# MLP weights split into high and low parts by two casting loads from GpSimd's queue

## Chip, core and metric

The kernel runs on one core of one Trainium2 chip. The metric is the device time of one execution in microseconds (us). Five engines work side by side, each through its own queue in order: TensorE (PE; its weight loads appear as PEld), VectorE (DVE), ScalarE (ACT), GpSimd (POOL) and SyncE (SP), which here only issues transfers (DMAs).

## What is computed

A trunk of two layers over 528 tokens (16 meta tokens and 512 of the input) of 1024 features. Each layer is a mixer (layer 0: retention and gated DeltaNet heads; layer 1: Mamba-2) followed by a squared-ReLU MLP with 4096 hidden features, each closed by a layer norm. The change is in the MLP:

```python
def sq_relu_mlp(h, w1, w2):
    return jnp.square(jax.nn.relu(h @ w1)) @ w2
...
    for i in range(DEPTH):
        ...
        h = layer_norm(DN_ALPHA * h + mix, ln1_w[i], ln1_b[i])
        h = layer_norm(DN_ALPHA * h + sq_relu_mlp(h, mlp_w1[i], mlp_w2[i]), ln2_w[i], ln2_b[i])
    return h[:, N_META:]
```

All inputs and the output are float32.

## The kernel before

Every large product is made of three matmuls in the float32r format (`mm3`): weight and activation are each held as a rounded high part and a low part that is the remainder, and high times high, high times low and low times high are added in PSUM.

**Weights.** They lie in HBM as tiles of 128 x 1024 float32 (512 KB): eight blocks of 128 x 128 side by side. `fetch` loads a tile from SP's queue into a raw buffer `wr` (2 buffers). `split` then makes the parts: ACT copies the raw tile with rounding into `wh`, and DVE subtracts that from the raw tile into `wl`. This goes by halves of 512 columns; `wh` and `wl` have 6 such halves each, which is three weight tiles. So SP is ahead of TensorE by up to two raw tiles and three split ones.

**The MLP.** `mlp` goes through the 4096 hidden features in four chunks of 1024. A chunk is a phase of eight `w1` tiles (each gives 128 hidden features for all tokens, f = 0 to 7), then a phase of eight `w2` tiles (each adds to 128 output features, m = 0 to 7). Two layers of four chunks of sixteen tiles are 128 weight tiles. Layer 0 works on 272 + 256 tokens as two halves, one PSUM tile `pmm` each; layer 1 works on 512 tokens in one. After a `w1` product `evac_u` takes it out for each half: ACT applies the ReLU (L381), GpSimd squares it in float32 (L383), ACT squares it with rounding into the high part (L389), DVE subtracts for the low part (L390). After a `w2` product DVE alone adds to the residual (L363, or L367 and L368).

**Ends of an MLP.** Its first three `w1` tiles (`head=3`) and its last three `w2` tiles (`tail=3`) are held together: the first half of the tokens goes through all three, and then the second half, so that the layer norm before or after can work on one half at a time. The layer norm ahead of the MLP uses GpSimd too: for a power of -0.5 (L147) and for the low parts `hl` of six of its eight feature tiles (L341).

**Order.** A tile scheduler sets the order of the instructions on each engine when the program is built, and adds the waits. In the queue of an engine nothing passes an instruction that waits. The weights of the mixers come through `wload` as well, and share the buffers `wh` and `wl` with the MLP.

Of the kernel before, what the change touches and what calls it, by code (L numbers as in the profile page):

```python
# [12 lines left out]
F32 = mybir.dt.float32  # L13
F32R = mybir.dt.float32r
# [4 lines left out]
P = 128  # L19
# [38 lines left out]
def trunk(ctx: ExitStack, tc: tile.TileContext, a, out):  # L58
# [7 lines left out]
    def nm(p):  # L66
        count[0] += 1
        return f"{p}{count[0]}"
# [23 lines left out]

    # ---------------------------------------------------------------- interleaving
    # The large products are cut into units; between two units every pending task (a generator) emits
    # its next stage, so that the tensor engine works on while other engines prepare a stage's inputs.
    tasks = []
# [29 lines left out]

    # ---------------------------------------------------------------- constants
    cst = one("cst", C_COLS)
# [20 lines left out]

    # ---------------------------------------------------------------- weights  # L150
    def split(dst_hi, dst_lo, src):
# [8 lines left out]
    def wload(src, n=1024, raw=None):  # L160
        if raw is None:
            raw = fetch(src, n)
        res = []
        for i in range(0, n, 512):
            c = min(512, n - i)
            hi = sb.tile([P, 512], F32R, tag="wh", bufs=6, name=nm("wh"))
            lo = sb.tile([P, 512], F32R, tag="wl", bufs=6, name=nm("wl"))
            split(hi[:, :c], lo[:, :c], raw[:, i:i + c])
            res.append((hi, lo))
        return res  # L170

    def mm3(o, w, x, first, last):
# [4 lines left out]
    def product(o, blks, xs, m=P, k0=0, k1=None, every=8):  # L177
        """o[m, n] += sum over k0 <= k < k1 of blks[k]^T xs[k]"""
        per = 512 // P if m == P else 8
        n = len(xs)  # L180
        for k in range(k0, k1 or n):
            hi, lo = blks[k // per]
            c = (k % per) * m
            mm3(o, (hi[:, c:c + m], lo[:, c:c + m]), xs[k], k == 0, k == n - 1)
            if k % every == every - 1 and k < n - 1:
                tick()

    def phase(tiles, rhs, evac, ns, head=0, tail=0, ready=None):
        """tiles: list of (srcs, key[, m]); rhs[half][k] = (hi, lo) APs, rhs[2] both halves where they fit a
        bank. In the first and the last tiles the halves are apart, so that what precedes and follows can  # L190
        work on one half at a time."""
        def both(blks, key):
            o = pm(512)
            product(o, blks, rhs[2], every=4)
            for hf in range(2):
                evac(key, hf, o[:, hf * 256:hf * 256 + 256])
            tick()

        def run(hf, blks, key, m=P):
            o = pm(ns[hf], part=m)  # L200
            product(o, blks, rhs[hf], m=m)
            evac(key, hf, o)
            tick()
        n = len(tiles)
        for i0, i1 in [(0, head)] + [(i, i + 1) for i in range(head, n - tail)] + [(n - tail, n)]:
            held = []
            for srcs, *key in tiles[i0:i1]:
                held.append(([b for s in srcs for b in (s if isinstance(s, list) else wload(s))], *key))
                if len(rhs) > 2 and head <= i0 < n - tail:
                    both(*held.pop())  # L210
                    continue
                if ready is not None and i0 == 0:
                    until(lambda: ready(0))
                run(0, *held[-1])
            if ready is not None and i0 == 0:
                until(lambda: ready(1))
            for args in held:
                run(1, *args)

    def jobs(lst, rhs, ns, **kw):  # L220
        """phase whose tiles bring their own evac"""
        phase(lst, rhs, lambda ev, hf, o: ev(hf, o), ns, **kw)

    # ---------------------------------------------------------------- h: hi/lo in two halves
    def htile():
        return [sb.tile([P, L], F32R, tag=f"h{kind}", bufs=8, name=nm(f"h{kind}")) for kind in "hl"]

    def parts(pair, spans):
        """(hi, lo) over the spans of both tiles"""
        return [tuple(x[:, o:o + n] for x in pair) for o, n in spans]  # L230

    # while the first loads are under way, products of zeros let the clock of the tensor engine come up
    zeros = tl("m", 272)
# [25 lines left out]
    def layernorm(r, ns, hf, go, apply, together=False):  # L259
        """statistics of the tokens of a half as its sums r come, then apply(off, bn, pt, mean, rstd, i)"""  # L260
        n = ns[hf]
# [48 lines left out]
    def norm_after(r, ns, wcol, bcol):  # L310
        """tasks for both halves, each from when its sums have been emitted"""
        res, pairs = [[], []], []
# [34 lines left out]
    def residual(hx, offs, ns, early=()):  # L347
        """evac into r = alpha * h + product"""
        r, pre = [{}, {}], [{}, {}]
# [23 lines left out]
    def mlp(l, hx, ns, ready, r, evac0):  # L373
        w1, w2 = a["mw1"], a["mw2"]
        for c in range(4):
            u = [[None] * 8 for _ in hx]

            def evac_u(f, hf, o):
# [5 lines left out]
                if hf == 0:  # L384
# [6 lines left out]

            phase([([w1[l, c * 8 + f]], f) for f in range(8)], hx, evac_u, ns,
                  head=3 if c == 0 else 0, ready=ready if c == 0 else None)
            phase([([w2[l, c, m]], m) for m in range(KT)], u,
                  lambda m, hf, o: evac0(m, hf, o, last=c == 3), ns, tail=3 if c == 3 else 0)

    # ---------------------------------------------------------------- shared pieces
    def conv_evac(cin, hf, o):
# [14 lines left out]
    def conv_job(src, wc, bcol, done):  # L413
        """projection through conv and silu, feature-major [128, L]"""
        cin = tl("s", L + 3)
        G.memset(cin[:, 0:3], 0.0)

        def evac(hf, o):
            conv_evac(cin, hf, o)
            if hf == 1:  # L420
                done(conv_silu(cin, wc, bcol))

        return [src], evac
# [21 lines left out]
    def gate_job(src, width, task):  # L445
        """small projection, then a task on its sums"""
        fm = tl("s", L, part=width)

        def evac(hf, o):
            off, n = HALF0[hf]  # L450
            S.copy(fm[:, off:off + n], o)
            if hf == 1:
                spawn(task(fm))

        return [src], evac, width

    def gate_task(fm, width):
        """token-major [128, 5, width] with unused rows zero"""
        pt = px(5 * width)
# [8 lines left out]
    def decay(dt_in, bias, alog, nh):  # L468
        """g = -exp(A_log) softplus(x + bias), sums over chunks and their exponentials"""
        n = 5 * nh  # L470
# [15 lines left out]

    # ================================================================ layer 0 mixer
    gd = {}
# [13 lines left out]

    # scratch in DRAM for the diagonal blocks of 32: a pitch of 129 rows makes the 68 blocks equidistant
    da, dt_, du = [dr.tile([17, 129, P], F32, tag=f"d{n}", bufs=1, name=f"d{n}") for n in "atu"]
# [25 lines left out]
    def gdn_keys(hd):  # L530
        yield
        yield from wait(lambda: "negc" in gd)
        f, gg, beta = kF[hd], gd["gg"], gd["beta"]
        # decays between the tokens of a chunk
        lg = tl("s", 512)
# [14 lines left out]
        V.tensor_tensor(e0, e0, triu[:16, 0:16], op=MUL)  # L550
        # similarities of the keys; the squared norms are on their diagonal
        pk = px(512)
# [31 lines left out]
    def gdn_base():  # L584
        """diagonal blocks of 32, one to a partition: forward substitution"""
        yield from wait(lambda: all(x is not None for x in AT))
# [347 lines left out]

    # ================================================================ layer 1 mixer
    lnf = sb.tile([P, 2048], F32, tag="cr", bufs=1, name="lnf")
# [26 lines left out]
    def hb(ap):  # L963
        """[128, heads] over the 64 features of a head"""
        return bc(ap, 64)
# [187 lines left out]
    hn, _, ready = norm_after(r, ns1, PP_LN + 32, PP_LN + 40)  # L1153
    # the first products begin with the groups that are ready
    until(lambda: yw[2][11] is not None)
# [19 lines left out]
    def finish(hf):  # L1175
# [16 lines left out]
        def last(blocks):  # L1192
            """both blocks at once, over the engines; what needs the mean alone comes first"""
            t = [[x[:, 0:512], x[:, 512:1024]] for x in (tl("row", 1024), tl("row", 1024))]
# [25 lines left out]

# ---------------------------------------------------------------- host side: layout only
def _tiles(w, cols):
    """[K, M] -> [M tiles, 128, K] in tiles of 128 columns"""
    k = w.shape[0]
    w = w[:, cols].reshape(k // P, P, -1, P)
    return np.ascontiguousarray(w.transpose(2, 1, 0, 3)).reshape(-1, P, k)
# [92 lines left out]
```

## Time and profile before

| | |
|---|---|
| device time, median of 3 runs | 1731.39 us (1730.09 to 1732.92) |
| span of the profiled execution, first to last instruction | 1727.4 us, 4.0 us below that median |
| TensorE busy | 1690.1 us, 98% |
| DVE, ACT, POOL busy | 1015.5, 680.0, 324.1 us |
| read from HBM | 149.95 MB, 90 GB/s over the span |
| MLP weight tiles loaded, on SP's queue | 128, from 495.4 to 1685.2 us |

The device time covers the span and what lies around it, so a sum is made against the span and 4.0 us are added for the time. Matmuls are pipelined: the duration of one is longer than the distance to the next, so the pace is read from what repeats once in a tile. The line numbers are those of the kernel before; in the changed kernel those from L164 on are ten higher (L383 becomes L393).

### The profile page before, as it was taken

The page shows a single profiled execution, that of the slowest core. Times are in us where ns is not written, and L with a number is a line of the kernel's source. Part 1 is how long each engine was busy: PE and PEld are TensorE (multiplying, and loading weights), DVE is VectorE, ACT ScalarE, POOL GpSimd, SP SyncE. Part 2 cuts the span into 40 slices and gives each one's busy share as a digit, 9 for nine tenths or more (in the row PEclk, how much of TensorE's full clock was granted, in tenths as well). Part 3 has the DMA queues.
Part 4 walks back from the last instruction along what each step waited for, and adds up shares of the span by engine and source line. Part 5 has one row for each costly group of instructions (what it writes and reads, how often), then busy time and mean ns, then how long its engine had stood idle before and what let it go on. Part 6 is the DMA issues. An engine that isn't in the chain of part 4 may idle for free.

```text
span 1727.4 us, 29456 instructions
## 1 busy us (share of the span) xinstructions
PE 1690.1 (98%) x11644; PEld 1537.0 (89%) x11644; DVE 1015.5 (59%) x2116; ACT 680.0 (39%) x1455; POOL 324.1 (19%) x380
## 2 busy tenths in 40 slices
PE   9999999999999999999999999999999999999997
PEld 8899998899999999999999878888788888888886
DVE  6896667676436443343348767868753744444345
ACT  4432345554225333242425634554432533333331
POOL 1311211010004111010202245242400411101012
PEclk9999999999999999999999999999999999999999
DMA  7224211112222222222221443333222222222221
GB/s 252 69 86 121 77 63 62 38 63 85 98 66 82 92 92 87 98 87 89 96 72 61 131 133 88 99 110 111 80 79 98 73 86 98 98 98 89 94 98 61
DMA packets 80325, 157.99 MB, mean 91 GB/s; under 512 B 12668, under 2 KB 45820, under 8 KB 79932
## 3 DMA queue, kind: packets, MB, share of 16 engines
q1 hardware_dynamic: 80044, 155.86, 28.2%
q8 instruction: 91, 1.49, 0.4%
q14 instruction: 46, 0.38, 0.1%
q10 hardware_dynamic: 144, 0.26, 0.0%
HBM read 149.95 MB, written 6.15 MB: 90 GB/s over the span
## 4 chain that ended last, share of the span: by engine, by line
PE 84%; DVE 6%; DMA 3%; POOL 3%; ACT 2%; issue 2%; SPq 0%; POOLq 0%; DVEq 0%; ACTq 0%
PE pmm L173 24%; PE pmm L175 24%; PE pmm L174 24%; DMA row<-rd 2%; DVE s L407 2%; DVE wl L153 2%; POOL row L985 1%; PE pmx L271 1%; POOL hl L341 1%; DMA wr<-in_w 1%; PE pmx L331 1%; PE pmx L1049 1%; PE pmx L1045 1%; POOL n L147 1%; PE pmx L753 1%
## 5 line engine op out<-in xcount | busy, mean ns | idle before, releaser
L173 PE MATMUL pmm<-hh,wh 128*128 128x272 f32 (+4 forms) x2104 | 652.3, 311 | 2.3 <-ACT wh L152 0.9
L174 PE MATMUL pmm<-hl,wh 128*128 128x272 f32 (+4 forms) x2104 | 638.5, 304 | 2.7 <-POOL hl L341 2.1
L175 PE MATMUL pmm<-hh,wl 128*128 128x272 f32 (+4 forms) x2104 | 640.3, 304 | 0.1
L153 DVE TENSOR_TENSOR wl<-wr,wh 128x512 fp32r<-128x512 f32 (+1 forms) x498 | 376.2, 759 | 319.8 <-ACT wh L152 313.5
L152 ACT CAST wh<-wr 128x512 fp32r<-128x512 f32 (+1 forms) x498 | 306.6, 619 | 628.3 <-PE pmm L174 605.1
L173 PEld LDWEIGHTS pmm<-hh,wh 128*128 128x128 f32 (+2 forms) x2104 | 393.5, 187 | 25.0 <-issue 4.4
L174 PEld LDWEIGHTS pmm<-hl,wh 128*128 128x128 f32 (+2 forms) x2104 | 393.6, 187 | 24.4 <-POOL hl L341 4.6
L175 PEld LDWEIGHTS pmm<-hh,wl 128*128 128x128 f32 (+2 forms) x2104 | 393.5, 187 | 17.0 <-DVE wl L153 0.3
L173 PE MATMUL pmm<-s,wh 128*128 128x256 f32 (+2 forms) x1192 | 377.9, 317 | 0.0
L175 PE MATMUL pmm<-s,wl 128*128 128x256 f32 (+2 forms) x1192 | 377.2, 317 | 0.0
L174 PE MATMUL pmm<-s,wh 128*128 128x256 f32 (+2 forms) x1192 | 376.4, 316 | 0.0
L174 PEld LDWEIGHTS pmm<-s,wh 128*128 128x128 f32 x1192 | 224.3, 188 | 15.5 <-DVE s L1124 0.3
L173 PEld LDWEIGHTS pmm<-s,wh 128*128 128x128 f32 x1192 | 224.4, 188 | 15.1
L175 PEld LDWEIGHTS pmm<-s,wl 128*128 128x128 f32 x1192 | 224.1, 188 | 15.0
L383 POOL TENSOR_TENSOR m<-m 128x256 f32<-128x256 f32 (+1 forms) x128 | 92.1, 729 | 536.0 <-ACT m L381 532.7
L147 POOL TENSOR_TENSOR n<-n,neg 128x1 f32<-128x1 f32 (+2 forms) x58 | 37.9, 657 | 462.7 <-DVE n L146 436.5
L390 DVE TENSOR_TENSOR s<-m,s 128x256 fp32r<-128x256 f32 (+1 forms) x128 | 64.3, 521 | 95.2 <-POOL m L383 93.2
L407 DVE SCALAR_TENSOR_TENSOR s<-s,pp,s 128x528 f32<-128x528 f32 x120 | 96.5, 804 | 25.8 <-ACT s L405 24.1
L363 DVE TENSOR_TENSOR m<-m,pmm 128x256 f32<-128x256 f32 (+1 forms) x108 | 43.7, 423 | 107.4 <-PE pmm L175 107.2
L381 ACT ACTIVATE m<-pmm 128x256 f32<-128x256 f32 (+1 forms) x128 | 48.7, 380 | 60.4 <-PE pmm L175 60.4
L985 POOL TENSOR_TENSOR row<-row,m 128x1024 f32<-128x1024 f32 x16 | 32.8, 2052 | 122.3 <-DMA row<-rd 78.3
L389 ACT ACTIVATE s<-m 128x256 fp32r<-128x256 f32 (+1 forms) x128 | 54.0, 422 | 3.9
(275 smaller groups left out, 1501.1 us busy)
## 6 DMA issues: line engine op xcount, KB each, us to landing
wr<-in_mw SPq DMA_DIRECT2D x128, 512.0 KB, 3.3
wr<-in_w SPq DMA_DIRECT2D x88, 512.0 KB, 3.3
wr<-in_wo SPq DMA_DIRECT2D x29, 512.0 KB, 3.5
row<-rd SPq DMA_DIRECT2D x16, 512.0 KB, 6.0
s<-rd SPq DMA_DIRECT2D x32, 128.0 KB, 6.1
out<-row SPq DMA_DIRECT2D x7, 256.0 KB, 2.0
wr<-in_wo SPq DMA_DIRECT2D x6, 256.0 KB, 3.0
dt<-row SPq DMA_DIRECT2D x3, 365.5 KB, 5.9
```

The source lines that it names most:

```text
L147: G.tensor_tensor(dst, t, neg5[0:part, 0:n], op=POW)
L152: S.copy(dst_hi, src)
L153: V.tensor_tensor(dst_lo, src, dst_hi.bitcast(F32), op=SUB)
L173: T.matmul(o, w[0], x[0], start=first, stop=False)
L174: T.matmul(o, w[0], x[1], start=False, stop=False)
L175: T.matmul(o, w[1], x[0], start=False, stop=last)
L381: S.activation(t, o, AF.Relu)
L383: G.tensor_tensor(q, t, t, op=MUL)
L389: S.activation(hi, t, AF.Square)
L390: V.tensor_tensor(lo, q, hi.bitcast(F32), op=SUB)
L407: V.scalar_tensor_tensor(acc, cin[:, k:k + L], w[k], acc, op0=MUL, op1=ADD)
L985: G.tensor_tensor(g3(rw, 8), g3(rw, 8), bc(gc[:, c * 32 + 8 * g:c * 32 + 8 * g + 8], P), op=SUB)
```

## The change

For the MLP, `wload` is replaced by a new `wcast`. It issues three instructions for a weight tile: a load from GpSimd's queue that casts the tile from HBM into `wh`; on ACT the negated high part into `wl`; and a second load of the same tile from GpSimd's queue that adds to `wl`. For the MLP there is no raw buffer, no load on SP's queue and no subtraction on DVE any more. The mixers keep `wload` and `split`. The buffers hold as many bytes as before, but come as 3 tiles of 1024 columns rather than 6 of 512, for the mixers too.

```diff
     def wload(src, n=1024, raw=None):
         if raw is None:
             raw = fetch(src, n)
+        hi = sb.tile([P, 1024], F32R, tag="wh", bufs=3, name=nm("wh"))
+        lo = sb.tile([P, 1024], F32R, tag="wl", bufs=3, name=nm("wl"))
         res = []
         for i in range(0, n, 512):
-            c = min(512, n - i)
-            hi = sb.tile([P, 512], F32R, tag="wh", bufs=6, name=nm("wh"))
-            lo = sb.tile([P, 512], F32R, tag="wl", bufs=6, name=nm("wl"))
-            split(hi[:, :c], lo[:, :c], raw[:, i:i + c])
-            res.append((hi, lo))
+            c = slice(i, min(i + 512, n))
+            split(hi[:, c], lo[:, c], raw[:, c])
+            res.append((hi[:, i:i + 512], lo[:, i:i + 512]))
         return res
+
+    def wcast(src, n=1024):
+        hi = sb.tile([P, 1024], F32R, tag="wh", bufs=3, name=nm("wh"))
+        lo = sb.tile([P, 1024], F32R, tag="wl", bufs=3, name=nm("wl"))
+        G.dma_start(hi[:, :n], src)
+        S.mul(lo[:, :n], hi[:, :n].bitcast(F32), -1.0)
+        G.dma_start(lo[:, :n], src, accum_op=ADD)
+        return [(hi[:, i:i + 512], lo[:, i:i + 512]) for i in range(0, n, 512)]
...
-            phase([([w1[l, c * 8 + f]], f) for f in range(8)], hx, evac_u, ns,
+            phase([([lambda f=f: wcast(w1[l, c * 8 + f])], f) for f in range(8)], hx, evac_u, ns,
                   head=3 if c == 0 else 0, ready=ready if c == 0 else None)
-            phase([([w2[l, c, m]], m) for m in range(KT)], u,
+            phase([([lambda m=m: wcast(w2[l, c, m])], m) for m in range(KT)], u,
```

(`phase` calls such a function where it called `wload` before.)

How the order changes on GpSimd is shown at three places. The first is the second chunk of layer 0, from the last `w1` products into the `w2` products. Before, the queue holds only the squares there (`m` is the ReLU and its square):

```order
L383 TENSOR_TENSOR m_8450<-m_8448 128x272
L383 TENSOR_TENSOR m_8483<-m_8481 128x256
L383 TENSOR_TENSOR m_8524<-m_8522 128x272
L383 TENSOR_TENSOR m_8557<-m_8555 128x256
L383 TENSOR_TENSOR m_9094<-m_9092 128x272
```

In the changed kernel the same place on GpSimd reads as follows (`wh` and `wl` are the parts of one weight tile, numbered alike but for the last digit; L177 is the casting load, L179 the adding one):

```order
L177 DMA wh_8370<-in_mw 128x1024
L393 TENSOR_TENSOR m_8276<-m_8274 128x272
L179 DMA wl_8371<-in_mw 128x1024
L393 TENSOR_TENSOR m_8309<-m_8307 128x256
L177 DMA wh_8427<-in_mw 128x1024
L177 DMA wh_8484<-in_mw 128x1024
L179 DMA wl_8428<-in_mw 128x1024
L179 DMA wl_8485<-in_mw 128x1024
L177 DMA wh_8541<-in_mw 128x1024
L179 DMA wl_8542<-in_mw 128x1024
L177 DMA wh_8598<-in_mw 128x1024
L179 DMA wl_8599<-in_mw 128x1024
```

Two loads for each tile now stand between and behind the squares, for the most part in the turn "cast a tile, add to the same tile, cast the next"; here and there two tiles are cast before either is added to.

The second place is the first chunk of layer 1, at the same point of a chunk. Before, on GpSimd:

```order
L383 TENSOR_TENSOR m_16458<-m_16456 128x256
L383 TENSOR_TENSOR m_16499<-m_16497 128x256
L383 TENSOR_TENSOR m_16507<-m_16505 128x256
L383 TENSOR_TENSOR m_16548<-m_16546 128x256
L383 TENSOR_TENSOR m_16556<-m_16554 128x256
```

In the changed kernel, on GpSimd:

```order
L177 DMA wh_15971<-in_mw 128x1024
L393 TENSOR_TENSOR m_15879<-m_15877 128x256
L177 DMA wh_16015<-in_mw 128x1024
L393 TENSOR_TENSOR m_15915<-m_15913 128x256
L179 DMA wl_15972<-in_mw 128x1024
L393 TENSOR_TENSOR m_15923<-m_15921 128x256
L179 DMA wl_16016<-in_mw 128x1024
L393 TENSOR_TENSOR m_15959<-m_15957 128x256
L177 DMA wh_16051<-in_mw 128x1024
```

Here the tiles come in pairs: both are cast before the first is added to, with squares of earlier products in between.

The third place is the entry into the MLP of layer 0, where the layer norm ends and the first three weight tiles are needed. Before, on GpSimd (`n` is the power in the layer norm):

```order
L147 TENSOR_TENSOR n_6513<-n_6514,neg_67 16x1
L147 TENSOR_TENSOR n_6526<-n_6527,neg_67 128x1
L147 TENSOR_TENSOR n_6594<-n_6595,neg_67 128x1
L341 TENSOR_TENSOR hl_6638<-m_6640,hh_6637 128x272
L341 TENSOR_TENSOR hl_6648<-m_6650,hh_6647 128x272
```

In the changed kernel, on GpSimd (of the six rows L351 three are shown, so two pieces):

```order
L177 DMA wh_6660<-in_mw 128x1024
L147 TENSOR_TENSOR n_6385<-n_6386,neg_67 16x1
L147 TENSOR_TENSOR n_6398<-n_6399,neg_67 128x1
L177 DMA wh_6759<-in_mw 128x1024
L147 TENSOR_TENSOR n_6466<-n_6467,neg_67 128x1
L179 DMA wl_6661<-in_mw 128x1024
L177 DMA wh_6797<-in_mw 128x1024
L351 TENSOR_TENSOR hl_6510<-m_6512,hh_6509 128x272
```

```order
L351 TENSOR_TENSOR hl_6550<-m_6552,hh_6549 128x272
L351 TENSOR_TENSOR hl_6560<-m_6562,hh_6559 128x272
L351 TENSOR_TENSOR hl_6570<-m_6572,hh_6569 128x272
L179 DMA wl_6760<-in_mw 128x1024
L179 DMA wl_6798<-in_mw 128x1024
```

The casting loads of the first three tiles stand among the powers of the layer norm, and the adding loads of the second and third tile behind all six `hl` rows.

More of the change, by code (lines that the diff above doesn't have):

```diff
@@ L207, in phase @@
             for srcs, *key in tiles[i0:i1]:
-                held.append(([b for s in srcs for b in (s if isinstance(s, list) else wload(s))], *key))
+                held.append(([b for s in srcs for b in (s if isinstance(s, list) else s() if callable(s) else wload(s))], *key))
                 if len(rhs) > 2 and head <= i0 < n - tail:
```

## The prediction

> **What bounds the kernel now.** I read the totals first, then the stretches of the two MLPs, and last the rows that repeat in every weight tile.
>
> ```profile
> span 1727.4 us, 29456 instructions
> PE 1690.1 (98%) x11644; PEld 1537.0 (89%) x11644; DVE 1015.5 (59%) x2116; ACT 680.0 (39%) x1455; POOL 324.1 (19%) x380
> ```
>
> TensorE is busy nearly throughout. By stretches of time (the columns are busy times of the five engines with counts of instructions, then TensorE's granted clock, the share of the 16 DMA engines and GB/s):
>
> ```profile
> 560.00:720.00 160.00, 160.00 (x1314) 160.00 (x1313) 68.01 (x126) 51.65 (x101) 16.95 (x23) 1.00 0.27 90
> 1400.00:1540.00 140.00, 140.00 (x605) 113.25 (x604) 61.00 (x117) 44.27 (x88) 12.67 (x18) 1.00 0.29 94
> ```
>
> ```profile
> 490.00:560.00 70.00, 68.67 (x537) 65.08 (x536) 40.60 (x89) 30.55 (x61) 20.20 (x26) 1.00 0.23 76
> 1300.00:1400.00 100.00, 98.43 (x566) 84.69 (x565) 53.26 (x111) 38.93 (x79) 22.59 (x30) 1.00 0.25 85
> 1690.00:1728.00 38.00, 26.41 (x198) 24.22 (x196) 21.18 (x50) 4.79 (x7) 10.14 (x10) 0.91 0.14 56
> ```
>
> Inside both MLPs TensorE has no idle time at all; where they begin it has 1.33 and 1.57 us, and at the kernel's end 11.6 us, in the last layer norm. So the 98% tell the reader where a gain could be: nowhere in the stretch that is changed, beyond some 3 us at its beginnings. What counts is whether weights still come in time. The pace shows in ACT's casts, whose idle time is ended by TensorE giving a buffer free (start, duration; layer 0, then layer 1):
>
> ```profile
> 599.53 0.62 ACT L152 CAST wh<-wr 128x512 fp32r<-128x512 f32 x1 [3.81 <-PE pmm L174]
> 605.38 0.62 ACT L152 CAST wh<-wr 128x512 fp32r<-128x512 f32 x1 [3.81 <-PE pmm L174]
> ```
>
> ```profile
> 1450.27 0.62 ACT L152 CAST wh<-wr 128x512 fp32r<-128x512 f32 x1 [2.15 <-PE pmm L174]
> 1450.80 0.38 ACT L381 ACTIVATE m<-pmm 128x256 f32<-128x256 f32 x1
> 1455.82 0.62 ACT L152 CAST wh<-wr 128x512 fp32r<-128x512 f32 x1 [2.15 <-PE pmm L174]
> ```
>
> The same cast comes again after 5.85 us in layer 0 and 5.55 us in layer 1: the time TensorE takes for a weight tile. A tile's preparation may hold each engine no longer than that, and from a free buffer to a finished tile there are two tiles' time (three buffers, one in use): 11.70 and 11.10 us. Before, all that lies between them is a cast and a subtraction, since the raw tile is already there.
>
> **The change, part by part.** What goes away: 256 casts and 256 subtractions of 128 x 512, and 128 issues on SP.
>
> ```profile
> L153 DVE TENSOR_TENSOR wl<-wr,wh 128x512 fp32r<-128x512 f32 x108 | 74.6, 690 | 111.6 <-ACT wh L152 111.6
> L152 ACT CAST wh<-wr 128x512 fp32r<-128x512 f32 x108 | 67.0, 620 | 191.0 <-PE pmm L174 191.0
> ```
>
> ```profile
> L157 SPq DMA_DIRECT2D wr<-in_mw x128: 327/328/328, 495.4 to 1685.2; - x128
> ```
>
> That is 256 x 0.69 = 177 us less on DVE and 256 x 0.62 = 159 us less on ACT, both worth nothing by themselves: TensorE waited for neither inside the stretches above. What comes: 128 negations of 128 x 1024 on ACT and 256 DMA issues on GpSimd. ACT and GpSimd rows near these in size:
>
> ```profile
> L986 ACT ACTIVATE row<-row 128x1024 f32<-128x1024 f32 x16 | 17.0, 1063 | 46.4 <-POOL row L985 44.8 <-POOL s L416 1.6
> ```
>
> ```profile
> L383 POOL TENSOR_TENSOR m<-m 128x256 f32<-128x256 f32 x96 | 71.7, 759 | 339.6 <-ACT m L381 338.2 <-issue 1.4
> L985 POOL TENSOR_TENSOR row<-row,m 128x1024 f32<-128x1024 f32 x16 | 32.8, 2052 | 122.3 <-DMA row<-rd 78.3 <-DVE s L407 37.0 <-PE pmm L174 5.0
> L147 POOL TENSOR_TENSOR n<-n,neg 128x1 f32<-128x1 f32 x48 | 29.1, 610 | 259.6 <-DVE n L146 242.8 <-DVE n L816 7.2 <-DVE n L307 7.0
> ```
>
> A negation is 1.06 us, so ACT gives back 128 x 1.06 = 136 us. The issues are what matters, and the trace has none on GpSimd. Three prices have to be bounded.
>
> *g, how long an issue holds GpSimd:* from 0.33 us (SP's issue) to 2.05 us (GpSimd's two-operand row on 128 x 1024). I take 1.0: starting anything there costs 0.61 us (one element per partition), and 128 rows have to be described by a program rather than by circuits.
>
> *From issue to landing*, by the page's list of DMA issues (KB each, median us to landing):
>
> ```profile
> wr<-in_mw SPq DMA_DIRECT2D x128, 512.0 KB, 3.3
> row<-rd SPq DMA_DIRECT2D x16, 512.0 KB, 6.0
> du<-row SPq DMA_DIRECT2D x3, 365.5 KB, 7.5
> ```
>
> The casting load moves what `wr<-in_mw` moves: between 3.3 and 6.0 us (the same bytes in short pieces). I take 3.3 + g = 4.3, as the rows must be described first. The adding load must also read the tile it adds to. One load a tile is 0.27 x 5.85 = 1.58 us of each DMA engine now, so a second reading adds as much: 4.3 + 1.58 = 5.9, within 4.3 and 7.5. The Trainium skill, page "Collectives: The Full Stack", section "The bandwidth ceiling: the fold count and why AG ≠ RS ≠ AR", says that a DMA which adds is slower by its two source reads and not by the addition; no run here shows it yet. By it the sum below stays as it is; if an adding load needed no second reading, the pairs and single turns of layer 1 and the pairs of layer 0 would lose about 65 us of it.
>
> Now the turns, by the order of the changed kernel. GpSimd runs in order, so the adding load, which waits for the negation, which waits for the casting load's landing, holds back all that stands behind it: squares, and the next tile's casting load. A handshake is 0.1 us:
>
> ```profile
> 1451.26 1.41 POOL L383 TENSOR_TENSOR m<-m 128x256 f32<-128x256 f32 x2 [48.78 <-ACT m L381]
> ```
>
> (ACT's ReLU above ends at 1450.80 + 0.38 = 1451.18.) From casting load to adding load are 4.3 + 0.1 + 1.06 + 0.1 = 5.56 us.
>
> - Layer 0, "cast, add, cast the next": 44 tiles. A turn lasts 5.56 + g = 6.56 us against TensorE's 5.85: 0.71 more, for 25 tiles: 18 us. In 19 of them a square stands behind the adding load: 0.76 + 0.71 = 1.47 more: 28 us. No lead absorbs it, since 5.56 + 5.9 = 11.46 of the 11.70 us are used anyway.
> - Layer 0, 9 pairs ("cast, cast, add, add"): the first adding load stands behind a casting load that waits until TensorE has left the tile before. It lands 0.1 + 1.0 + 5.9 = 7.0 us after that; TensorE wants it after 5.85: 1.15 x 9 = 10 us.
> - Layer 1, 23 pairs: 7.0 - 5.55 = 1.45 for the 7 without squares (10 us), and 0.76 more, 2.2, for the 16 with one in front of the adding load (35 us). 14 single turns among them: the cast is issued only when the pair's last adding load has been, 0.1 + 5.56 + 1.0 = 6.66 us after a buffer came free and so 1.11 after the next one did; with the chain of 11.46 it lands 1.11 + 11.46 - 11.10 = 1.47 late: 20 us.
> - Collisions: a tile is three readings, 3 x 1.58 = 4.7 us of every DMA engine in a turn of about 7. In the 44 single turns of layer 0 a casting load is issued while the adding load still moves. From 0 to 2 us; I take 0.5: 22 us.
> - Ends: at each entry the second and third adding loads stand behind the six `hl` rows, which wait for the layer norm, where before the raw tiles lay ready:
>
> ```profile
> 522.31 4.61 POOL L341 TENSOR_TENSOR hl<-m,hh 128x272 fp32r<-128x272 f32 x6 [2.67 <-DVE m L340]
> ```
>
>   A load issued after 526.9 lands 5.9 later, at about 533; in a `head` TensorE asks for a tile every 3 us. At each tail three tiles are asked for at 3 us intervals while GpSimd delivers one in 6.6. About 5 us at each of four ends, 20 us; from 0 to 40.
>
> The casting loads' waits for free buffers, and squares that come late, cost nothing further: a phase's products need the last hidden features last, 7/8 of a tile's time later, and `w2` products are taken out by DVE, which is idle more than half of the time. The mixers' coarser buffers cost nothing: cast and subtraction of a whole tile, about 2 us, have 11 us there too.
>
> Sum: 18 + 28 + 10 + 10 + 35 + 20 + 22 + 20 = 163 us on the span of 1727.4, so 1890; with the 4.0 us by which the median of the runs stands above it, 1894. With all prices at their lower ends (g 0.33, 3.3 and 3.3) a turn is 4.89 us and nothing stalls: 1731. With all at the upper (2.05, 6.0, 7.5, ends 40; collisions are in so long a landing, and layer 1's single turns counted as plain pairs): 25 x 3.46 + 19 x 4.22 + 9 x 3.80 + 16 x 4.86 + 21 x 4.10 + 40 = 405: 2136.
>
> **Rivals.** *It fits.* If a load issued by GpSimd lands as soon as SP's, 3.3 us, and an issue costs 0.61, a turn is 3.3 + 1.26 + 0.61 = 5.17, with a square 5.93, and a pair's first tile lands after 4.0 or 4.8: only the ends cost, 0 to 20 us. Halfway to my prices it is some 50 us, so this case reaches from 1731 to 1785, with 1743 its centre. For it speaks that bytes and rows are those of `wr<-in_mw`; against it that GpSimd's smallest rows are already twice SP's issue. The Trainium skill, page "DMA: Bandwidth & Descriptors", section "Anatomy of one DMA — SWDGE (gpsimd) path", has this case: 2.0 us plus bytes / 436e3, which for 512 KB is an estimate of 3.2 us, with little for describing; the trace agrees for SP's loads (3.3) and has none of GpSimd's.
>
> *The converting or adding transfer is slow* (short pieces, or arithmetic in the DMA engine), and lands after 7.5 us or more: 2000 to 2136 or beyond by the upper ends. For it speaks `row<-rd`, whose 512 KB take 6.0 us; against it that the rows here are 4 KB long.
>
> *Faster.* DVE and ACT lose 177 and 23 us of work, and the idle time at the beginnings, 1.33 + 1.57 us, ends on them. It decides only if GpSimd's turn stays below 5.55 us and the adding loads at the entries come in time too: 1728.5.
>
> **How the numbers follow.** The stall in nearly every turn (1785 to 2000): 0.63. It fits: 0.20. Slow transfer: 0.14. Faster: 0.03. A measurement of this kernel can tell 0.2% from no change, 3.5 us; of "it fits" a quarter lies within that, 0.05. So faster 0.03, same 0.05, slower 0.92. The range leaves out about 0.1 on each side, half of "it fits" and part of the slow transfers: 1755 to 2060.
>
> **What would show it.** GpSimd's issues should read near 1.0 us, the casting load land after about 4.3 and the adding one after about 5.9. TensorE should wait for the adding load (`wl`) about 160 us in all, in gaps of 1 to 2 us in most tiles, larger with a square in the turn and at the four ends; the DMA share in the MLPs should rise from 0.27 to about 0.65, DVE's busy time fall by 177 us, and all other stretches stay as they are. I am wrong if TensorE stays at 160.00 of 160.00 inside the MLPs (prices near the lower ends), or if its gaps exceed 3 us everywhere: then the adding transfer is slow. Should the granted clock fall below 1.00 in these gaps, that adds a cost I have not priced.

## The result

The changed kernel takes 1928.09 us (median of 4 runs, 1919.58 to 1934.42) against 1730.74 us before (4 runs on the same chip): a ratio of 1.1138, 95% interval 1.1107 to 1.1168, or 197 us more. The forecast was 1894 us, slower, with a range of 1755 to 2060.

### The profile page after: what moved, and what is told of

It is laid out like the page before. It is cut to its first block, busy times and chain, and to the rows that moved or that the text cites. A ratio compares the mean times of both kernels' runs of the same rounds, so it can differ in the third digit from the quotient of the medians.

```text
span 1932.6 us, 28997 instructions
## 1 busy us (share of the span) xinstructions
PE 1759.3 (91%) x11644; PEld 1582.6 (82%) x11644; DVE 823.1 (43%) x1860; ACT 651.1 (34%) x1327; POOL 492.5 (25%) x636
## 5 line engine op out<-in xcount | busy, mean ns | idle before, releaser
L185 PE MATMUL pmm<-hh,wl 128*128 128x272 f32 (+4 forms) x2104 | 657.6, 313 | 67.3 <-DMA wl<-in_mw 67.1
L183 PE MATMUL pmm<-hh,wh 128*128 128x272 f32 (+4 forms) x2104 | 667.6, 317 | 3.4 <-ACT s L410 0.7
L184 PE MATMUL pmm<-hl,wh 128*128 128x272 f32 (+4 forms) x2104 | 651.6, 310 | 0.5 <-DVE hl L153 0.2
L185 PEld LDWEIGHTS pmm<-hh,wl 128*128 128x128 f32 (+2 forms) x2104 | 405.4, 193 | 94.9 <-DMA wl<-in_mw 77.1
L185 PE MATMUL pmm<-s,wl 128*128 128x256 f32 (+2 forms) x1192 | 388.5, 326 | 62.5 <-DMA wl<-in_mw 62.5
L183 PE MATMUL pmm<-s,wh 128*128 128x256 f32 (+2 forms) x1192 | 385.2, 323 | 0.0
L184 PE MATMUL pmm<-s,wh 128*128 128x256 f32 (+2 forms) x1192 | 384.4, 323 | 0.5 <-DVE s L400 0.5
L178 ACT ACTIVATE wl<-wh 128x1024 fp32r<-128x1024 f32 x128 | 135.6, 1059 | 550.8 <-DMA wh<-in_mw 549.6
L185 PEld LDWEIGHTS pmm<-s,wl 128*128 128x128 f32 x1192 | 231.0, 194 | 89.0 <-DMA wl<-in_mw 74.2
L184 PEld LDWEIGHTS pmm<-s,wh 128*128 128x128 f32 x1192 | 231.0, 194 | 16.5 <-DVE s L400 0.7
L183 PEld LDWEIGHTS pmm<-s,wh 128*128 128x128 f32 x1192 | 231.1, 194 | 14.7
L153 DVE TENSOR_TENSOR wl<-wr,wh 128x512 fp32r<-128x512 f32 (+1 forms) x242 | 183.0, 770 | 118.7 <-ACT wh L152 114.9
L152 ACT CAST wh<-wr 128x512 fp32r<-128x512 f32 (+1 forms) x242 | 144.6, 616 | 240.6 <-PE pmm L184 219.1
L179 POOL DMA_DIRECT2D wl<-in_mw x128 | 113.1, 886 | 400.7 <-ACT wl L178 326.7
L177 POOL DMA_DIRECT2D wh<-in_mw x128 | 90.3, 705 | 336.3 <-PE pmm L185 213.8
```

Source lines behind the costliest of these rows:

```text
L152: S.copy(dst_hi, src)
L153: V.tensor_tensor(dst_lo, src, dst_hi.bitcast(F32), op=SUB)
L177: G.dma_start(hi[:, :n], src)
L178: S.mul(lo[:, :n], hi[:, :n].bitcast(F32), -1.0)
L179: G.dma_start(lo[:, :n], src, accum_op=ADD)
L183: T.matmul(o, w[0], x[0], start=first, stop=False)
```

## The profile after

First the page of the changed kernel: totals, and the idle time in front of the groups that matter (after the bar: busy us, mean ns of one, then idle us before it and what ended the idle time).

```profile
span 1932.6 us, 28997 instructions
PE 1759.3 (91%) x11644; PEld 1582.6 (82%) x11644; DVE 823.1 (43%) x1860; ACT 651.1 (34%) x1327; POOL 492.5 (25%) x636
L185 PE MATMUL pmm<-hh,wl 128*128 128x272 f32 (+4 forms) x2104 | 657.6, 313 | 67.3 <-DMA wl<-in_mw 67.1
L185 PE MATMUL pmm<-s,wl 128*128 128x256 f32 (+2 forms) x1192 | 388.5, 326 | 62.5 <-DMA wl<-in_mw 62.5
L178 ACT ACTIVATE wl<-wh 128x1024 fp32r<-128x1024 f32 x128 | 135.6, 1059 | 550.8 <-DMA wh<-in_mw 549.6
L179 POOL DMA_DIRECT2D wl<-in_mw x128 | 113.1, 886 | 400.7 <-ACT wl L178 326.7
L177 POOL DMA_DIRECT2D wh<-in_mw x128 | 90.3, 705 | 336.3 <-PE pmm L185 213.8
wh<-in_mw POOLq DMA_DIRECT2D x128, 512.0 KB, 5.5
wl<-in_mw POOLq DMA_DIRECT2D x128, 512.0 KB, 5.4
```

DVE and ACT have less to do than before, GpSimd more (492.5 us instead of 324.1), but GpSimd is busy for 25% of the time only. TensorE is idle for 1932.6 - 1759.3 = 173.3 us against 1727.4 - 1690.1 = 37.3. Of that, 129.6 us end on the adding load (`wl<-in_mw`, the two L185 rows). GpSimd stands still 326.7 us in front of its adding loads until the negation has run, and ACT stands still 549.6 us in front of the negations until the casting load has landed. So the chain is to be read backwards: TensorE waits for the adding load, GpSimd for ACT, ACT for the casting load.

Where it lies, by stretches: the two MLPs of the changed kernel, then the same two of the kernel before (from the first to the last of the MLP's matmuls; columns as in the prediction).

```profile
526.20:1024.80 498.60, 422.20 (x3140) 411.47 (x3138) 87.13 (x202) 124.56 (x210) 141.50 (x207) 0.93 0.59 134
1472.60:1920.70 448.10, 389.96 (x1732) 313.00 (x1730) 80.83 (x195) 119.51 (x202) 142.42 (x204) 0.95 0.66 148
```

```profile
522.00:908.10 386.10, 384.85 (x3140) 382.25 (x3139) 171.13 (x331) 138.02 (x277) 60.24 (x83) 1.00 0.27 87
1349.40:1715.80 366.40, 365.07 (x1738) 301.79 (x1736) 169.27 (x324) 127.94 (x265) 60.57 (x81) 1.00 0.27 89
```

Layer 0's MLP takes 498.6 - 386.1 = 112.5 us more, layer 1's 448.1 - 366.4 = 81.7, and all the rest 11.0: the two profiled spans differ by 1932.6 - 1727.4 = 205.2, and 194.2 of that lie in the MLPs. Inside the MLPs it is not idle time alone: TensorE's busy time grows by 37.4 and 24.9 us for the same matmuls, and the granted clock is 0.93 and 0.95 where it was 1.00.

The turn itself, in the `w2` phase of layer 0's first chunk: GpSimd's and ACT's timelines (start, duration; in brackets the idle time before and what ended it).

```profile
619.25 0.86 POOL L179 DMA_DIRECT2D wl<-in_mw  x1 [5.31 <-ACT wl L178]
619.80 0.88 POOL L177 DMA_DIRECT2D wh<-in_mw  x1
627.32 0.86 POOL L179 DMA_DIRECT2D wl<-in_mw  x1 [6.64 <-ACT wl L178]
627.87 0.88 POOL L177 DMA_DIRECT2D wh<-in_mw  x1
```

```profile
617.89 1.06 ACT L178 ACTIVATE wl<-wh 128x1024 fp32r<-128x1024 f32 x1 [7.12 <-DMA wh<-in_mw]
625.96 1.06 ACT L178 ACTIVATE wl<-wh 128x1024 fp32r<-128x1024 f32 x1 [7.01 <-DMA wh<-in_mw]
```

One turn, from adding load to adding load, is 627.32 - 619.25 = 8.07 us: 0.55 to the next casting load, 6.16 until ACT can start (625.96), 1.06 for the negation, 0.30 back to GpSimd. TensorE needs 5.85. All 42 single turns of layer 0 in this trace have a median of 8.35 us. Nothing but the waiting fills GpSimd's queue in the turn shown: the bracket on each adding load is the wait itself, and the casting load behind it starts at once, with no wait for a buffer. Elsewhere it does wait for one: in front of 47 of the 128 casting loads, 29 of them in layer 1, where most tiles come in pairs.

## The experiments

Four theories, by the names that the expectations use. *Turn:* GpSimd's queue is held from a tile's casting load to its adding load, so tiles come one turn apart. *Chain:* the way from a free buffer to a finished tile (cast, negate, add) is too long for three buffers, whatever the order. *DMA load:* three readings for each tile crowd the DMA engines. *Clock:* TensorE is slowed by its own gaps. Runs of three rounds or more have an interval; the others are one run each, beside a kernel before of 1729.9 to 1731.1 us.

### The buffers alone

All MLP tiles go through `wload` as before; of the change only the three buffers of 1024 columns are left.

```diff
-            phase([([lambda f=f: wcast(w1[l, c * 8 + f])], f) for f in range(8)], hx, evac_u, ns,
+            phase([([lambda f=f: wload(w1[l, c * 8 + f])], f) for f in range(8)], hx, evac_u, ns,
...
-            phase([([lambda m=m: wcast(w2[l, c, m])], m) for m in range(KT)], u,
+            phase([([lambda m=m: wload(w2[l, c, m])], m) for m in range(KT)], u,
```

> The MLP's weights come through wload again (raw load from SP, cast on ACT, subtraction on DVE); of the change only the coarser buffers remain, 3 tiles of 1024 columns instead of 6 of 512. Every theory that puts the loss into GpSimd's loads expects the time of before, 1731 us within 4. A rival that blames the buffers (a tile's cast can start only when TensorE has left the whole tile before it) expects a good part of the loss here, 1760 or more.

Measured 1730.78 us, ratio 1.0003 (0.9994 to 1.0013). The coarser buffers cost nothing.

### One GpSimd load at a time

With the adding load alone, the high part is cast by ACT from a raw load on SP's queue:

```diff
-        G.dma_start(hi[:, :n], src)
+        raw = fetch(src, n)
+        S.copy(hi[:, :n], raw[:, :n])
```

> The high part is cast on ACT from a raw tile loaded from SP again, the negation stays on ACT, and only the adding load is issued by GpSimd. Theory 'turn' (GpSimd's queue is held from the issue of the casting load until its tile has landed and been negated, and that sets the pace): the holding is gone, one issue of 0.88 us per tile remains, and from a free buffer to a finished tile are 1.06 + 1.06 + 0.2 + 5.4 = 7.7 us of 11: 1733 to 1750, the rest at the two entries. Theory 'DMA load' (three readings per tile on the 16 DMA engines, 58% busy, make everything late): the DMA engines have the same to do, so 1850 or more.

With the casting load alone, the low part is a subtraction on DVE from a raw load on SP's queue:

```diff
+        raw = fetch(src, n)
         G.dma_start(hi[:, :n], src)
-        S.mul(lo[:, :n], hi[:, :n].bitcast(F32), -1.0)
-        G.dma_start(lo[:, :n], src, accum_op=ADD)
+        V.tensor_tensor(lo[:, :n], raw[:, :n], hi[:, :n].bitcast(F32), op=SUB)
```

> Only the casting load is issued by GpSimd; the low part is the difference of a raw tile (loaded from SP as before) and the high part, on DVE over 1024 columns. Theory 'turn': nothing on GpSimd waits for a landing, chain 3.4 + 0.1 + 1.4 = 5 us: 1731 to 1742. A rival by which the issue of a load on GpSimd, or a cast in the DMA engines, is slow in itself expects 1780 or more.

Measured 1751.49 us, ratio 1.0108 (1.0087 to 1.0129), and 1733.19 us, ratio 1.0008 (0.9998 to 1.0017). The middle of layer 0's MLP, first with the adding load alone, then with the casting load alone:

```profile
600.00:760.00 160.00, 160.00 (x1314) 160.00 (x1313) 28.80 (x67) 74.76 (x108) 40.23 (x54) 1.00 0.82 180
```

```profile
600.00:760.00 160.00, 160.00 (x1314) 160.00 (x1313) 60.84 (x91) 23.65 (x58) 33.49 (x56) 1.00 0.56 182
```

TensorE is busy for 160.00 of 160.00 us in both: neither load alone makes it wait inside an MLP. With the adding load alone the DMA engines work 0.82 of the time, more than in the changed kernel (0.59), and nothing stalls there: the load on the DMA engines as such is not the cause. Of its remaining 20 us 17 lie at the entries and tails of the MLPs, read from the first and last matmul of each phase in the traces: the first phase of layer 0 takes 60.6 us instead of 55.6, the last 54.0 instead of 49.6, the first of layer 1 58.3 instead of 50.9.

### A second load that overwrites

The adding load becomes a plain load into the same tile, in the same place and with the same wait. The addition is left out, so the low part is not the remainder.

```diff
-        G.dma_start(lo[:, :n], src, accum_op=ADD)
+        G.dma_start(lo[:, :n], src)
```

> The second load overwrites the negated part instead of adding to it (the subtraction is left out); order of all instructions, waits and bytes read from HBM are those of the change. Theory 'turn with collisions' (the casting load lands late, 5.5 instead of 3.4 us, because it moves behind an adding load whose packets take 328 ns instead of 174): the second load takes 1.4 instead of 2.6 us of each DMA engine, casting loads land after about 4.2 us, a turn in layer 0 is about 6.1 to 6.8, pairs in layer 1 fit: 1770 to 1810. Theory 'turn, by the order alone': landing times change little and 1890 or more remain. Theory 'clock' (TensorE's half-rate stretches cost most): follows whatever the gaps do, the clock back to 0.98 or more.

Measured 1788.96 us. GpSimd's turns there, and the landings:

```profile
614.25 0.53 POOL L179 DMA_DIRECT2D wl<-in_mw  x1 [5.38 <-ACT wl L178]
614.77 0.54 POOL L177 DMA_DIRECT2D wh<-in_mw  x1
620.64 0.53 POOL L179 DMA_DIRECT2D wl<-in_mw  x1 [5.33 <-ACT wl L178]
```

```profile
wh<-in_mw POOLq DMA_DIRECT2D x128, 512.0 KB, 4.4
wl<-in_mw POOLq DMA_DIRECT2D x128, 512.0 KB, 3.6
```

The order and the waits are those of the changed kernel; the turn shown is 6.39 us instead of 8.07 (medians of the single turns of layer 0: 7.03 and 8.35), and the casting load lands after 4.4 us instead of 5.5, the medians of all 128. For the casting loads issued less than 1 us behind a second load, counted in the two traces, the medians are 4.5 and 6.2 us. So in the single turns the adding load does its harm by what it does to the casting load issued 0.55 us behind it: that landing is inside the turn, its own is not. The 139 us between this kernel and the changed one are the price of adding. The 58 us that stay are the turn without it, together with the ends: TensorE is idle for 5.9 of the 160 us from 600 to 760 us here, and the first and last phase of each MLP take some 18 us more than before; some 10 us lie outside the MLPs.

### More buffers, and a later need

Four buffers instead of three, for `wh` and `wl`, in `wload` and in `wcast` (one line of the four):

```diff
...
-        hi = sb.tile([P, 1024], F32R, tag="wh", bufs=3, name=nm("wh"))
+        hi = sb.tile([P, 1024], F32R, tag="wh", bufs=4, name=nm("wh"))
...
```

> Four weight tiles in the buffers instead of three; all else as in the change, and the order on GpSimd in layer 0 is still mostly 'cast, add, cast the next'. Theory 'turn' (GpSimd is held from each casting load to the adding load of the same tile): no help in layer 0, where the turn of about 7.4 us stays above TensorE's 5.85, so about 47 us to spare per chunk stay lost there: some 100 us in layer 0; in layer 1 the casting load in front of a pair's first adding load waits for a tile less, so most of its 80 us go: 1820 to 1870. Theory 'chain' (too few tiles prepared ahead): one more tile of lead, 1745 to 1790.

Each product of a full MLP tile takes its eight matmuls with `wl` last, so that TensorE asks for `wl` only when two thirds of the product are done:

```diff
+            for k in range(2 * n):
...
+                if k < n:
+                    T.matmul(o, hi[:, c:c + m], xs[k][0], start=k == 0, stop=False)
+                    T.matmul(o, hi[:, c:c + m], xs[k][1], start=False, stop=False)
+                else:
+                    T.matmul(o, lo[:, c:c + m], xs[k - n][0], start=False, stop=k == 2 * n - 1)
```

> TensorE uses the low part last: all products with the high part of a tile, then all with the low part, so the low part is wanted 2/3 of a tile (3.9 and 3.7 us) later and a high part's buffer is free 1.9 us earlier; loads and waits on GpSimd are those of the change, in an order that differs a little. Theory 'turn': a lead of 3.9 us is used up once per run of single turns and does not change the pace of layer 0; layer 1, which is bound by when a tile lands after the one before, gains: 1820 to 1880. Theory 'chain': the tiles come in time, 1745 to 1790.

Measured 1865.48 us and 1879.66 us. Both help a little and neither cures: a longer lead or a later need shifts each tile once, but where tiles come at a turn's pace the stall returns with every tile. With four buffers the single turns of layer 0 are as long as before the edit, 8.36 us at the median. With four buffers, 600 to 760 us:

```profile
600.00:760.00 160.00, 136.42 (x1046) 133.73 (x1045) 24.20 (x57) 34.26 (x54) 42.59 (x62) 0.96 0.63 144
```

The chain theory, which wanted 1745 to 1790 us here, falls as the cause of the whole. It has a part in layer 1: in the six phases between an MLP's first and last one, 74 of 82 us of the loss stay in layer 0, but only 30 of 52 in layer 1, where most tiles come in pairs.

### The adding load without its wait

The negation reads a constant tile, so it need not wait for the casting load, and the adding load no longer holds GpSimd's queue. Bytes, issues and additions stay; the low part is not the remainder.

```diff
-        S.mul(lo[:, :n], hi[:, :n].bitcast(F32), -1.0)
+        S.mul(lo[:, :n], still[0][:, :n], -1.0)
```

> ACT negates a constant tile that lies in SBUF instead of the high part, so the adding load no longer waits for the casting load's landing (the low part is then not the remainder); loads, bytes, buffers and the negation's length stay, and GpSimd's order is 'cast, add' throughout. Theory 'turn': GpSimd is held for 0.62 + 0.88 us per tile only, and the DMA engines have 1.4 + 2.6 = 4.0 us to do in 5.85: 1735 to 1760. Theory 'DMA load' (readings collide whatever the order): casting loads still land late and 1850 or more remain.

Measured 1751.56 us. The middles of both MLPs:

```profile
600.00:760.00 160.00, 160.00 (x1313) 160.00 (x1313) 28.95 (x67) 47.46 (x79) 56.01 (x81) 1.00 0.85 180
1440.00:1580.00 140.00, 140.00 (x607) 113.59 (x607) 22.94 (x59) 41.78 (x73) 52.20 (x75) 1.00 0.90 191
```

All the stall inside the MLPs is gone with one dependence, while the DMA engines carry 0.85 to 0.90, so the theory of the DMA load falls here too. The edit does two things, though: GpSimd's queue is not held any more, so that the scheduler writes "cast, add" for every tile, and the way from a free buffer to a finished tile is shorter, since the negation need not wait for the casting load. Which of the two counts is told by the four buffers: a longer lead alone left most of the loss and the turn's length as they were. The two runs together show the turn.

### More work for TensorE

In layer 0 each product of the first half repeats its first matmul six times, about 0.75 us more TensorE work for a tile (48 us in all). If the turn sets the pace, it should be hidden.

```diff
+            for _ in range(fill if k == 0 else 0):
+                T.matmul(o, hi[:, c:c + m], xs[k][0], start=True, stop=True)
```

> In layer 0's MLP TensorE gets six repeats of the first product of each weight tile, in front of the place where it waits for the low part: 64 x 6 x 0.126 = 48 us of work that changes no result and that shortens its idle gaps, so that the clock should fall to half rate less often. GpSimd's order in layer 0 becomes 'cast, add, cast the next' for nearly all tiles; layer 1 is as in the change. Theory 'turn': the gaps take the extra work and the pace stays GpSimd's, 59 to 62 us for a phase of eight tiles in layer 0 (59.6 in the change): 1915 to 1950. Theory 'clock': without the half-rate stretches the phases of layer 0 fall to 57 or less: 1890 to 1910. If TensorE itself were the bound, 1960 or more.

(`fill` is 6 for the first half in layer 0, and 0 elsewhere.) Measured 1971.51 us, ratio 1.1395 (1.1374 to 1.1415): a miss for the first two. By its number it would be the third, but that is not what the trace shows; TensorE still waits:

```profile
600.00:720.00 120.00, 102.30 (x794) 99.05 (x792) 18.46 (x43) 24.70 (x41) 27.84 (x41) 0.99 0.57 131
```

```profile
622.41 0.87 POOL L179 DMA_DIRECT2D wl<-in_mw  x1 [6.69 <-ACT wl L178]
622.95 0.89 POOL L177 DMA_DIRECT2D wh<-in_mw  x1
630.57 0.87 POOL L179 DMA_DIRECT2D wl<-in_mw  x1 [6.73 <-ACT wl L178]
631.11 0.88 POOL L177 DMA_DIRECT2D wh<-in_mw  x1
```

The turn is 630.57 - 622.41 = 8.16 us, as before the edit. What changed is the order that the scheduler wrote: counted in the two traces, GpSimd's queue in layer 0 has 2 places where two tiles are cast before either is added to, and 60 single turns with a median of 8.16 us; the changed kernel has 11 and 42, median 8.35. A pair spends one wait on two tiles: in the changed kernel 10.9 us at the median, where two single turns take 16.7. Nine pairs fewer are some 9 x 5.8 = 52 us by this estimate, about as much as the 48 us that were added. The expectation had foreseen the new order, but not its price: it kept the 59.6 us of a phase with pairs in it, while eight single turns of 8.16 us are 65.3, and the phases of layer 0 take 64.3 to 70.6 between the first and the last. So single turns do hide TensorE's additional work, and what was lost is, by this estimate, the pairs. The run also bounds the clock: here it was granted at 0.99 in this stretch, and the median of the single turns is the same within 0.2 us.

### Casting ahead

The casting load of a tile is issued two tiles ahead of its adding load, with five high buffers; no sum is left out.

```diff
+    def wcast(srcs, started, i, n=1024):
+        for j in range(len(started), min(i + 3, len(srcs))):
+            hi = sb.tile([P, 1024], F32R, tag="wh", bufs=5, name=nm("wh"))
+            G.dma_start(hi[:, :n], srcs[j])
+            started.append(hi)
+        hi = started[i]
...
```

> The casting load is issued two tiles ahead of the adding load: five buffers for high parts (three for low parts as in the change), the loads, the negation and all waits of a tile on its own parts as in the change. When the adding load comes up on GpSimd its casting load has long landed. Theory 'turn': the queue is not held any more, a turn is 0.62 + 0.88 us and a square, the chain from a free low buffer is 1.06 + 0.2 + 5.4 = 6.7 us of 11: 1735 to 1760, the rest at the ends. Theory 'DMA load': as many readings in the same time, 1850 or more.

Measured 1758.34 us, ratio 1.0154 (1.0136 to 1.0173). Inside the MLPs nothing stalls, and the loads land as follows:

```profile
600.00:760.00 160.00, 160.00 (x1314) 160.00 (x1314) 29.77 (x69) 46.02 (x75) 54.41 (x79) 1.00 0.85 180
```

```profile
wh<-in_mw POOLq DMA_DIRECT2D x128, 512.0 KB, 3.6
wl<-in_mw POOLq DMA_DIRECT2D x128, 512.0 KB, 5.8
```

The casting load lands 1.9 us sooner than in the changed kernel; the adding one a little later, but nobody waits for it so soon. Every wait of a tile on its own parts is as in the changed kernel and every sum is kept; what differs is the order and the two buffers that it needs. Since four buffers in the old order cured little, it is the order that cures, with the room that it needs.

Three more runs ask where the 28 us that stay come from. First, the first and last three tiles of each MLP go through `wload`:

> The casting load is issued two tiles ahead as in the run before, and at each MLP's two ends (the first three and the last three weight tiles) the weights come as before the change: raw load from SP, cast, subtraction. If what is left of the loss with loads cast ahead (28 us) lies at the four ends, where GpSimd's rows of the layer norm and three tiles at double pace meet, 1732 to 1742; if it lies in the coarser or differently shared buffers outside the MLPs, 1750 or more stays.

Measured 1753.67 us, ratio 1.0145 (1.0128 to 1.0162): the weight loads at the ends are not the larger part. Then five high buffers with every tile split as before, and last the kernel with `wload` at the ends, but with the two additional buffers under a tag of their own that the mixers don't use (`wload` has three again):

```diff
-            hi = sb.tile([P, 1024], F32R, tag="wh", bufs=5, name=nm("wh"))
+            hi = sb.tile([P, 1024], F32R, tag="wh" if j % 5 < 3 else "wc", bufs=3 if j % 5 < 3 else 2, name=nm("wh"))
```

> Every weight tile is split by ACT and DVE from one raw load, as before; the only change against the kernel before is the buffers: tiles of 128 x 1024 with five high and three low ones. The runs with casting loads two tiles ahead kept some 25 us, and in their traces these lie in the mixers' stretches, not in the MLPs. If the five high buffers are what costs there (weights fetched and cast further ahead, in another order with the mixers' own work): 1745 to 1758 us. If the loss needs GpSimd's DMA issues or the moved layer-norm work beside them: 1729 to 1735 us.

> As the run with casting loads two tiles ahead and the first and last three tiles of each MLP split by ACT and DVE, but the two additional high buffers are used by casting loads of the MLPs alone; the mixers have three and three. If the five buffers in the mixers cost the rest: 1730 to 1738 us, that is the time before, with 116 of 128 tiles split by GpSimd's loads. If the rest comes from something else: 1748 to 1758 us. Should the adding load hold GpSimd back even here (the turn as in the changed kernel), more than 1800 us.

Measured 1750.62 us, ratio 1.0120 (1.0103 to 1.0137), and 1739.15 us, ratio 1.0053 (1.0038 to 1.0068). With five buffers and no GpSimd load at all, the MLP's own raw loads (first and last start in us) come late:

```profile
L157 SPq DMA_DIRECT2D wr<-in_mw x128: 327/328/328, 509.7 to 1710.2; - x128
```

Before, they started at 495.4 and 1685.2: the first 14.3 us later, the last 25.0. The two MLPs take 385.3 and 364.2 us, as with three buffers (385.4 and 364.9). So five buffers in the mixers account for some 20 us: there the scheduler puts the mixers' own small matmuls and the weight tiles in another order, and TensorE waits more in the first mixer (busy for 246.98 of its first 260 us, and 253.12 before). With the mixers back at three, 116 of 128 tiles split by GpSimd cost 0.5%, and TensorE has no idle time in the middle of either MLP:

```profile
600.00:760.00 160.00, 160.00 (x1313) 160.00 (x1313) 28.34 (x66) 47.72 (x81) 56.37 (x81) 1.00 0.84 180
1400.00:1540.00 140.00, 140.00 (x606) 113.56 (x605) 25.60 (x67) 39.19 (x65) 49.34 (x71) 1.00 0.88 190
```

No version came out faster than the kernel before; TensorE bounds it, and the work taken off DVE and ACT is worth nothing there. Why 0.5% stay (5.4 us of it before the first MLP begins, by the trace) was not tried.

## Why the prediction was right, and where its sizes were off

**What bounds it, and the mechanism: right.** The adding load holds GpSimd's queue until negation and casting load are done, and tiles then come slower than TensorE uses them. Issuing the casting loads two tiles ahead, so that nothing is waited for when the adding load comes up, takes away the stall inside the MLPs with every sum kept; a fourth buffer in the old order does not.

**g, 1.0 us: too high.** An issue holds GpSimd for 0.55 us to the next instruction (619.25 to 619.80); its span reads 0.71 (casting) and 0.89 us (adding) on average. Both ends of the bound, 0.33 and 2.05, hold.

**Casting load, 4.3 us: wrong in its base.** Undisturbed it lands after 3.6 us. The rival "it fits", with 3.3, was nearer in this piece. The Trainium skill, page "DMA: Bandwidth & Descriptors", section "Anatomy of one DMA — SWDGE (gpsimd) path", gives an estimate of 3.2 us for 512 KB by its formula; the runs show 3.6 for the casting load with nothing close ahead of it.

**Collisions, 0.5 us a tile: the term that was too small.** In the 42 single turns of layer 0 the casting load lands after 6.1 us at the median, 2.5 more than undisturbed. Against the 4.3 of the prediction that is 1.8, inside its bound of 2; against the measured 3.6 it is outside. The errors in g, landing and collision partly cancel: 1.0 + 4.3 + 0.5 + 1.06 + 0.2 = 7.06 predicted for a turn against 0.55 + 6.16 + 1.06 + 0.30 = 8.07 in the one shown. By the median of 8.35 a single turn costs 8.35 - 5.85 = 2.5 us, 105 us for the 42, where the forecast had 18 + 28 + 22 = 68.

**Pairs in layer 0, 10 us: too dear.** A pair takes 10.9 us at the median, and TensorE needs 11.7 for two tiles, so the pairs cost nothing. That is part of why layer 0 is short by only 112.5 - 88 = 24.5 us (78 + 10 with half of the ends).

**Adding load, 5.9 us: near.** Its median is 5.4 us, and 5.8 where casting loads stand close ahead of it. That it takes as much of the DMA engines' time as two loads is shown by the DMA share at one and the same pace of TensorE: 0.27 with one load a tile (before), 0.56 with two (casting load and raw load), 0.85 with a casting and an adding load: 0.28 to 0.29 for each load, and the adding load counts for two. That the second share is a reading of the tile it adds to is the prediction's argument; no run sets reading and adding apart. The rule of the Trainium skill, page "Collectives: The Full Stack", section "The bandwidth ceiling: the fold count and why AG ≠ RS ≠ AR", that an addition costs its two source reads, agrees with the doubled share.

**Layer 1, 10 + 35 + 20 + 10 = 75 us: near in its sum, by luck:** 81.7 measured. Its 15 single turns have a median of 8.5 us, 2.9 above TensorE's 5.55: 41 us for the forecast's 14, twice the 20 that it had. Its pairs take 12.6 us at the median, 1.5 above two tiles' 11.1: 34 us for 23, where it had 45.

**Ends, 20 us: right in size,** as far as a run with no stall inside the MLPs shows it: 17 us with the adding load alone. In the changed kernel itself ends and turns mix.

**The slow transfer: refuted,** since neither load needs 7.5 us at the median. **Buffers, 0: right** for three of 1024 columns. **DMA share 0.65:** 0.59 and 0.66. **DVE -177 us:** -192.4, since a subtraction costs 192.4 / 256 = 0.75 us and not the 0.69 of the row that I took. **TensorE's waits for `wl`, 160 us:** 129.6; most of the rest of the loss came as slower matmuls.

**Not priced: the clock.** TensorE's busy time grew by 69 us. The prediction named this cost as one it had not priced. How much of this is on the path isn't settled. In single turns TensorE only waits less when it works slower; in pairs and in layer 1 it may count. And 11 us lie outside the MLPs, where the prediction had none; their cause stays open.

## What to carry to other kernels

Before a transfer is moved to another engine's queue, write down what the queue does while the transfer's data are waited for: a load that waits for the product of an earlier load on the same queue turns overlapped loads into turns. The cure is order (issue the first step of a later tile ahead of the waiting step), more than buffers. And when buffers are shared by two parts of a program, giving more to one can reorder the other.

## What was not expected of the hardware

- An adding load slows the load issued right behind it. It lands after 5.4 us itself; a casting load issued less than 1 us behind it lands after 6.2 us at the median, behind a plain load after 4.5, and with nothing close ahead after 3.6. Casting in the transfer costs next to nothing: 3.6 us against 3.3 for a raw load on SP's queue.
- DMA engines busy 0.85 to 0.90 of the time in an MLP did not disturb TensorE at all, as long as nothing waited in turn.
- Gaps of 2 us are mostly followed by a halved clock. In the trace of the changed kernel TensorE's clock is granted at half rate in 34 stretches of 3.4 us or a multiple, 136.5 us together; before, there were 3, of 18.9 us. The difference of 117.6 us is at most 59 us of lost work, most of the 69 by which the busy time grew. Of 37 gaps of 2.0 us or more, 27 are followed by such a stretch within 3.5 us (of the 33 below 3.4 us, 23); of 45 gaps of 0.3 to 1.5 us, 5. These are counts from one trace; no run varied the gaps alone. The Trainium skill, page "TensorE: Matmul & The Clock Gate", section "Part 1: The HAM clock gate (the "warmup" mystery)", gives the half rate after an idle window of some 3.4 us; the stretches have that length here, but most of the gaps ahead of them are shorter.
- The number of buffers reached a part of the program that the edit didn't touch: five high ones instead of three made the mixers some 20 us slower with no other change.
